# The sixteen extra tokens of an expert mixer: their copies, transposes and scalings placed behind query projection 9

## The chip, the cores and the metric

The kernel runs on one core of one Trainium2 chip. The metric is the device time of one execution in microseconds (us). The kernel before was timed three times: 1357.75 us in the median, 1357.3 to 1359.09.

## The reference

The reference computes one inference step of a hybrid decoder layer in float32, for 336 tokens of width 1024: 16 learned meta tokens and 256 prompt tokens of one sequence, and 8 running sequences of 8 tokens. A Conformer convolution branch and a Mamba-2 branch share an input projection; their gated sum goes through an output projection and is added to the input. The outputs include the new convolution caches and the recurrent states. Behind that stands the PEER expert mixer, which is the part that matters here:

```python
q = (xb @ w_q).reshape(T, PEER_HEADS, 2, D_KEY // 2)
s = jnp.einsum('thcd,hckd->thck', q, keys).astype(jnp.float32)
s1, i1 = lax.top_k(s[:, :, 0], PEER_TOPK)
s2, i2 = lax.top_k(s[:, :, 1], PEER_TOPK)
...
sc, f = lax.top_k(cand, PEER_TOPK)
...
g = jax.nn.softmax(sc, axis=-1)
act = jax.nn.gelu(jnp.einsum('thkd,td->thk', U[ids], xb).astype(jnp.float32), approximate=False)
w = (g * act).astype(xb.dtype)
return jnp.einsum('thk,thkd->td', w, V[ids])
```

Each token is normalised, projected to 8 heads of two 128-wide half queries, scored against 128 keys per half, and gets 16 of 16384 experts per head. Each chosen expert contributes a row of V, weighted by the softmax weight times the gelu of a dot product with a row of U. The result is added to the token and normalised once more. The outputs do not hold the meta tokens, so 320 tokens go through the mixer.

## The kernel before

**Stages.** The first 540 us or so compute the two branches and the output projection. Then come 16 query projections (one per head and half), with scores and top-16 searches, and then the experts. The 320 tokens are treated in two ways. For 176 of them (ND) the experts are computed densely: 128 blocks of U (`u_block`, L1274) give a matrix S of gelu values for all experts, which is masked with the softmax weights (`g_step`, L1303 to L1310), and 128 blocks of V are summed up in PSUM (`v_block`, L1368). For the other 144 tokens the chosen rows of U and V are gathered from HBM by indirect DMAs. 128 tokens (NGAT) sit one in each partition and take 128 gathers, one per head and choice. The last 16 tokens (NX), the extra tokens, sit in eight copies each in the 128 partitions (partition = copy x 16 + token), so that 16 further gathers serve all their 128 choices. 144 gathers in all, 1 MB each (L1085), each followed by a product with the token summed along the row (L1197), a gelu and a scaling (L1199, L1200), and a weighted sum (L1205).

**What the extra tokens need ahead of their gathers.** `x2e` holds the normalised extra tokens in eight copies, token by partition, and `acce` the sum that the gathers add to, at first zero except for the raw tokens in the first 16 partitions. The tokens lie feature by partition in `xT`. So POOL repeats 16 columns eight times into a 128 x 128 tile `xe` (L988, eight times, two buffers), PE transposes it into the PSUM tile `px` (L990, four into each of two tiles), ACT copies 16 partitions of it to `acce` (L991), and DVE scales it into `x2e` by the token's inverse norm and the weights row `n2r` (L992). The inverse norms are turned the same way: POOL copies them into `xe` (L979), PE multiplies by a column of the identity into column 3 of the PSUM tile `prs` (L981), and ACT copies that to `rsT` (L982). POOL also clears `acce` (L977). The gathered 128 tokens have the same steps ahead of these (L964 to L971), with columns 0 to 2 of `prs`.

**Query projections.** `weight` (L245) loads a 128 x 1024 slice of w_q by SP, ACT casts it to a high part `wh` (L219), and POOL takes the difference as a low part `wl` (L220, one in ten on DVE); `wh` and `wl` have two buffers each. `proj` runs 24 matmuls into a PSUM tile `pj` (L152, three buffers). ACT copies it to `qT` (L1104, three buffers). Three score matmuls (L1107) write the PSUM tile `psc`, one for each token tile, and ACT copies each out (L1109); for the gathered tokens DVE finds the top 16 at once (`top16`, L999 to L1007). Behind projections 7 and 15, `heads` turns the searches of four heads into expert numbers `gid` and weights `ggw`. Behind projection 7 the first four gathers are asked for (`ahead(0)`). The gathers' buffers `wuv` are five; `n2r` is held in one of them until its last reader is done.

**PSUM.** The tiles px, prs and psc all come from one tag with two buffers:

```python
def misc(shape, name):
    return ps.tile(shape, F32, name=name, tag="misc", bufs=2)
```

**Order.** The order on each engine is set when the program is built, by a planner that runs a model of the machine: at each moment an engine takes, among the instructions whose inputs and buffers are ready, the one that stands first in the program text. So work may be pulled ahead into gaps. On the chip each engine then runs its list strictly in order. In the stage in question the PE's order is left to the planner (`pin[0] = False`); in the branches before it, PE's order is that of the text.

Of the kernel before, what the change touches and what calls it, by code (L numbers as in the profile page):

```python
# [38 lines left out]
NX = 16  # L39
# [3 lines left out]
NCOL = NPICK + (NPICK // XQ if NX else 0)  # L43
XAT = 64
HG = 4
LEAD = 4
GT = 8
SB = 88
# [89 lines left out]
def body(tc, ia, oa, stop=None):  # L138
    nc = tc.nc
    with ExitStack() as top:  # L140
# [58 lines left out]
        def pj(name="pj"):  # L199
            return ps.tile([128, PJ], F32, name=name, tag="pj", bufs=3)[:, :T]  # L200

        def pj2(name="pj"):
            return pj(name)[:, :T2]
# [39 lines left out]
        def weight(src, i):  # L243
            raw = wp.tile([128, KD, 128], F32, name="wraw", bufs=rb[0])
            nc.sync.dma_start(raw, src[i].rearrange("p (k m) -> p k m", m=128))  # L245
            h = wp.tile([128, KD, 128], F32R, name="wh", bufs=2)
            l = wp.tile([128, KD, 128], F32R, name="wl", bufs=2)
            nw[0] += 1
            f_ = lm[0]
            on_dve = int((nw[0] + 1) * f_) > int(nw[0] * f_)  # L250
            split(h, l, raw, on_pool=not on_dve, on_dve=lm[0] == 1)
            return h, l
# [6 lines left out]
        def misc(shape, name):  # L259
            return ps.tile(shape, F32, name=name, tag="misc", bufs=2)  # L260
# [64 lines left out]
        p = misc([128, T], "pn1")  # L325
# [569 lines left out]
        for j in range(KD):  # L895
# [4 lines left out]
            p = pj2()  # L900
# [7 lines left out]
        for j in range(KD):  # L908
            w = weight(ia["w_o"], j)
            p = pj2()  # L910
# [13 lines left out]
        p = ps.tile([128, T], F32, name="pn2", tag="pb", bufs=1)  # L924
# [36 lines left out]
        for c_ in range(2):  # L961
            p = misc([128, 512], "px")
# [4 lines left out]
        p = misc([128, 4], "prs")  # L967
# [4 lines left out]
        for k in range(KD):  # L972
            nc.vector.scalar_tensor_tensor(nd[:, k, :], xT[:, k, NGAT:NGAT + ND], V("n2", k), rs2[:, NGAT:NGAT + ND],
                                           op0=OP.mult, op1=OP.mult)
        if NX:
            E0 = NGAT + ND
            nc.gpsimd.memset(acce, 0.0)  # L977
            xe = qp.tile([128, 128], F32, name="xe", bufs=2)
            nc.gpsimd.tensor_copy(xe.rearrange("p (q t) -> p q t", t=NX),  # L979
                                  rs2[:, None, E0:T2].to_broadcast([128, XQ, NX]))  # L980
            nc.tensor.matmul(p[:, 3:4], xe, ident[:, 0:1], start=True, stop=True)  # L981
            nc.scalar.copy(rsT[:, 3:4], p[:, 3:4])  # L982
            for c_ in range(2):
                p = misc([128, 512], "px")
                cs = slice(c_ * 512, c_ * 512 + 512)
                for k in range(4):
                    xe = qp.tile([128, 128], F32, name="xe", bufs=2)
                    nc.gpsimd.tensor_copy(xe.rearrange("p (q t) -> p q t", t=NX),  # L988
                                          xT[:, 4 * c_ + k, None, E0:T2].to_broadcast([128, XQ, NX]))
                    nc.tensor.transpose(p[:, k * 128:(k + 1) * 128], xe, ident)  # L990
                nc.scalar.copy(acce[:NX, cs], p[:NX])  # L991
                nc.vector.scalar_tensor_tensor(x2e[:, cs], p, rsT[:, 3:4], n2r[:, cs], op0=OP.mult, op1=OP.mult)  # L992
# [4 lines left out]
        def top16(vals, idx, v, h, late=False):  # L997
            L = v.shape[0]
            i_ = nc.vector.max(vals[:L, h, 0:8], v)  # L999
            if late:  # L1000
                tc.add_manual_dep(i_.ins, early[0], mybir.DependencyInfo(mybir.DependencyClass.NoSync,
                                                                         mybir.DependencyReason.DATA),
                                  reason="gathered tokens first")
            nc.vector.max_index(idx[:L, h, 0:8], vals[:L, h, 0:8], v)
            nc.vector.match_replace(v, vals[:L, h, 0:8], v, -3.0e38)
            nc.vector.max(vals[:L, h, 8:16], v)
            nc.vector.max_index(idx[:L, h, 8:16], vals[:L, h, 8:16], v)  # L1007
# [7 lines left out]
        def candidates(L, H_, s2):  # L1015
            c = kp.tile([128, PH * 136], F32, name="cand", bufs=1)[:L]
            cf = c[:, :H_ * 136].rearrange("p (h n) -> p h n", h=H_)
            nc.vector.tensor_tensor(cf[:, :, :16], s2[:, :, 0, 0:1].to_broadcast([L, H_, 16]), s2[:, :, 1, :],
                                    op=OP.add)
            nc.vector.tensor_tensor(cf[:, :, 16:].rearrange("p h (a b) -> p h a b", b=8),  # L1020
                                    s2[:, :, 0, 1:, None].to_broadcast([L, H_, 15, 8]),
                                    s2[:, :, 1, None, :8].to_broadcast([L, H_, 15, 8]), op=OP.add)
            return c, cf

        def table(L, H_, idx):
            sf = kp.tile([128, PH, 2, 16, 4], BF, name="sf", bufs=2)[:L, :H_]
            nc.vector.tensor_copy(sf.rearrange("p h c k t -> p (h c k) t"),
                                  idx.rearrange("p h k -> p (h k)")[:, :, None].to_broadcast([L, H_ * 32, 4]))
            return sf

        def places(L, H_, f):
            lo = kp.tile([128, PH * 16], U32, name="plo")[:L, :H_ * 16]
            rr = kp.tile([128, PH * 16], U32, name="prr")[:L, :H_ * 16]
            ab = [kp.tile([128, PH * 16], BF, name=f"pab{c_}")[:L, :H_ * 16] for c_ in range(2)]
            nc.vector.tensor_scalar(lo, f, 7, None, op0=OP.bitwise_and)
            nc.vector.tensor_scalar(rr, f, 3, None, op0=OP.logical_shift_right)
            nc.vector.tensor_scalar(ab[0], rr, 1.0, 0.0, op0=OP.subtract, op1=OP.max)
            nc.vector.tensor_scalar(ab[1], rr, 1.0, 8.0, op0=OP.is_equal, op1=OP.mult)
            nc.vector.tensor_tensor(ab[1], ab[1], lo, op=OP.add)
            return ab  # L1040
# [14 lines left out]
        def heads(h0):  # L1055
            hs_ = slice(h0, h0 + HG)
            cs = slice(16 * h0, 16 * (h0 + HG))
            sf = table(128, HG, si[0][:, 2 * h0:2 * h0 + 2 * HG])
            c, cf = candidates(128, HG, sv[0].rearrange("p (h c) k -> p h c k", c=2)[:, hs_])
            for h in range(HG):  # L1060
                top16(cv0, ci0, cf[:, h], h0 + h)
            ab = places(128, HG, ci0.rearrange("p h k -> p (h k)")[:, cs])
            pk = kp.tile([128, 2, HG * 16], F32, name="pkh")
            for half in range(2):
                look(pk[:, half], 128, HG, ab[half], sf, half, c)
            idf = kp.tile([128, HG * 16], F32, name="idh")
            nc.vector.scalar_tensor_tensor(idf, pk[:, 0], float(NK), pk[:, 1], op0=OP.mult, op1=OP.add)
            early.append(nc.vector.tensor_copy(gid[:, cs], idf).ins.name)
            g_ = kp.tile([128, HG, 16], F32, name="gh")
            nc.vector.tensor_tensor(g_, cv0[:, hs_], cv0[:, hs_, 0:1].to_broadcast([128, HG, 16]), op=OP.subtract)  # L1070
            act(g_, g_, AF.Exp, scale=rsT[:, 0:1])
            sm = kp.tile([128, HG], F32, name="smh")
            nc.vector.tensor_reduce(sm, g_, axis=AX.X, op=OP.add)
            nc.vector.reciprocal(sm, sm)
            nc.vector.tensor_tensor(ggw[:, cs].rearrange("p (h k) -> p h k", k=16), g_,
                                    sm[:, :, None].to_broadcast([128, HG, 16]), op=OP.mult)
# [6 lines left out]
        def gather(c):  # L1083
# [3 lines left out]
            steps = ustep[SB:] + vstep  # L1087
            if len(steps) > LEAD:
                tc.add_manual_dep(i_.ins, steps[-1 - LEAD], mybir.DependencyInfo(mybir.DependencyClass.Sync,
                                                                          mybir.DependencyReason.DATA),  # L1090
# [8 lines left out]
        for j in range(16):  # L1099
            w = weight(ia["w_q"], j)  # L1100
            p = pj()
            proj(p[:, :T2], w, rows(ah[:, :, :T2], al[:, :, :T2]))
            qT = qp.tile([128, T], F32, name="qT", bufs=3)
            nc.scalar.copy(qT[:, :T2], p[:, :T2])  # L1104
            p = misc([128, 3, NK], "psc")
            for i, (t0, L) in enumerate(KTILES):
                nc.tensor.matmul(p[:L, i], qT[:, t0:t0 + L], keys[:, j, :], start=True, stop=True)  # L1107
                s_ = sall[:, i - 1, j] if i else kp.tile([128, NK], F32, name="sco", bufs=9)
                nc.scalar.copy(s_[:L], p[:L, i])  # L1109
                if i == 0:  # L1110
                    top16(sv[i], si[i], s_[:L], j)
            if j % (2 * HG) == 2 * HG - 1:
                heads(j // 2 - HG + 1)
            if j == 2 * HG - 1:
                ahead(0)
# [386 lines left out]
```

## Time and profile before

| | |
|---|---|
| median of three runs | 1357.75 us (1357.3 to 1359.09) |
| the profiled execution | 1359.33 us |
| its span | 1357.6 us |
| PE busy | 1316.2 us (97%) |
| DVE busy | 1017.4 us (75%) |
| ACT busy | 526.4 us (39%) |
| POOL busy | 576.2 us (42%) |
| transferred | 382.05 MB, mean 281 GB/s |

The profile is of one execution. Its page gives busy times, the span in 40 slices and the chain of work that ended last; the trace behind it can be asked for stretches, for single tiles and lines, for who waited for whom, and for each engine's instructions in order of time. PE is TensorE's matmuls, PEld its weight loads, DVE VectorE, ACT ScalarE, POOL GpSimd, SP SyncE, which issues DMAs. A line "a<-b" means that the instruction writes a and reads b; L988 is line 988 of the kernel. An idle time in brackets is that of the engine ahead of the instruction, with what ended it. One float32 matmul stands as two instructions in the trace where its operands are plain float32 (psc, px, prs).

### The profile page before, as it was taken

Reading aid. Unit: us, or ns where it says so; the run is one execution under the profiler, and the core shown is the slowest. Engines: PE = TensorE matmul, PEld = TensorE weight load, DVE = VectorE, ACT = ScalarE, POOL = GpSimd, SP = SyncE. Lnnn points to the kernel's source line nnn. Section 1 sums busy time; section 2 is a strip of 40 time slices with the busy share of each in tenths; the row PEclk is TensorE's granted clock in tenths of the full one; section 3 lists DMA queues with packets and bytes.
Section 4 is the critical chain, followed back from the end, with each engine's and each line's share of the span. In section 5 each row is a group of like instructions: output and inputs, shape, how many; then the busy total and the mean of one; then the engine's idle time right before and its main releaser. Section 6 shows DMA issues by size and latency. Waiting matters only on the chain.

```text
span 1357.6 us, 24599 instructions
## 1 busy us (share of the span) xinstructions
PE 1316.2 (97%) x9324; PEld 1247.7 (92%) x9324; DVE 1017.4 (75%) x2340; ACT 526.4 (39%) x1393; POOL 576.2 (42%) x492
## 2 busy tenths in 40 slices
PE   9999999999999999999999998999999999989997
PEld 7888888888889999898998998999999999988997
DVE  7888777877877236789999986877877878765544
ACT  6777877778666444442232121121111101110012
POOL 2477776776665667542221331222222221332210
PEclk9899999999999999999999998999999999999999
DMA  6434554454343444628999999999999999999994
GB/s 239 156 125 168 169 176 129 148 166 172 128 138 126 156 144 155 193 94 316 392 415 412 394 415 414 374 409 378 379 403 415 386 375 383 382 417 414 415 415 170
DMA packets 87094, 382.05 MB, mean 281 GB/s; under 512 B 10144, under 2 KB 15648, under 8 KB 66368
## 3 DMA queue, kind: packets, MB, share of 16 engines
q1 hardware_dynamic: 65056, 227.46, 45.9%
q0 software_dynamic: 20736, 151.00, 27.5%
q10 hardware_dynamic: 1184, 2.02, 0.4%
q8 instruction: 73, 1.20, 0.4%
q14 instruction: 45, 0.37, 0.1%
HBM read 367.41 MB, written 13.03 MB: 280 GB/s over the span
## 4 chain that ended last, share of the span: by engine, by line
PE 74%; DVE 12%; DMA 11%; ACT 2%; issue 1%; POOL 0%; ACTq 0%; DVEq 0%; SPq 0%
PE pj L152 30%; PE va L1368 16%; PE pj L1274 14%; DMA eraw<-in_vE_dram 7%; PE pg L1303 4%; DMA eraw<-in_uT_dram 3%; PE pst L152 2%; DVE wuv L1197 1%; DVE ygat L1205 1%; PE po L152 1%; PE py L152 1%; DVE pcv L475 1%; PE pdec L152 1%; PE psc L1107 1%; PE ptr L157 1%
## 5 line engine op out<-in xcount | busy, mean ns | idle before, releaser
L1085 POOL DMA_INDIRECT wuv<-in_peer_uv_dram,gid x144 | 178.0, 1236 | 522.9 <-DVE ygat L1205 203.8
L1274 PE MATMUL pj<-nd,eraw 128*128 128x176 f32 x2048 | 324.1, 319 | 9.3 <-DMA eraw<-in_uT_dram 5.5
L220 POOL TENSOR_TENSOR wl<-wraw,wh 128x1024 fp32r<-128x1024 f32 x111 | 267.1, 2407 | 151.8 <-ACT wh L219 79.2
L1368 PE MATMUL va<-S,eraw 128*128 128x176 f32 x2048 | 315.5, 314 | 8.5 <-DMA eraw<-in_vE_dram 8.3
L1274 PEld LDWEIGHTS pj<-nd,eraw 128*128 128x128 f32 x2048 | 313.0, 194 | 11.5 <-ACT S L1276 6.2
L1368 PEld LDWEIGHTS va<-S,eraw 128*128 128x128 f32 x2048 | 306.0, 190 | 13.6 <-DMA eraw<-in_vE_dram 11.1
L152 PE MATMUL pj<-ah,wh 128*128 128x336 f32 (+1 forms) x768 | 244.4, 329 | 0.7 <-ACT xnf L195 0.7
L152 PE MATMUL pj<-al,wh 128*128 128x336 f32 (+1 forms) x768 | 234.5, 318 | 0.0
L1205 DVE SCALAR_TENSOR_TENSOR ygat<-wuv,scg,ygat 128x1024 f32<-128x1024 f32 x128 | 163.9, 1280 | 48.7 <-ACT scg L1200 48.5
L1199 ACT ACTIVATE scg<-scg 128x1 f32<-128x1 f32 x144 | 29.0, 202 | 429.3 <-DVE wuv L1197 429.2
L1197 DVE SCALAR_TENSOR_TENSOR wuv<-wuv,x2m 128x1024 f32<-128x1024 f32 x128 | 155.9, 1218 | 47.3 <-DMA wuv<-in_peer_uv_dram,gid 47.3
L219 ACT CAST wh<-wraw 128x1024 fp32r<-128x1024 f32 x125 | 131.1, 1050 | 117.6 <-PE pj L152 79.9
L475 DVE SCALAR_TENSOR_TENSOR pcv<-ccat,vec,pcv 128x256 f32<-128x256 f32 x464 | 148.7, 379 | 17.1 <-ACT pcv L473 17.1
L152 PEld LDWEIGHTS pj<-ah,wh 128*128 128x128 f32 x768 | 147.4, 192 | 8.6 <-ACT xnf L195 2.7
L152 PEld LDWEIGHTS pj<-al,wh 128*128 128x128 f32 x768 | 147.0, 192 | 0.7
L152 PE MATMUL pj<-ah,wl 128*128 128x336 f32 (+1 forms) x768 | 137.1, 316 | 0.0
L152 PEld LDWEIGHTS pj<-ah,wl 128*128 128x128 f32 x768 | 120.8, 189 | 0.8 <-issue 0.7
L1276 ACT ACTIVATE S<-pj 128x176 f32<-128x176 f32 x128 | 37.5, 311 | 141.8 <-PE pj L1274 141.7
L1303 PE MATMUL pg<-oh 128*128 128x64 bf16 x1056 | 75.0, 241 | 0.0
L1303 PEld LDWEIGHTS <-oh 128*128 128x128 bf16 x1056 | 70.9, 117 | 2.2
L1310 DVE TENSOR_TENSOR S<-S,pg 128x192 f32<-128x192 f32 (+1 forms) x66 | 31.6, 506 | 54.9 <-PE pg L1303 54.8
L489 DVE SCALAR_TENSOR_TENSOR pj<-mcat,vec,pj 128x360 f32<-128x360 f32 x96 | 56.2, 587 | 3.7 <-ACT pj L487 3.7
(366 smaller groups left out, 1701.7 us busy)
## 6 DMA issues: line engine op xcount, KB each, us to landing
eraw<-in_uT_dram SPq DMA_DIRECT2D x128, 512.0 KB, 10.0
eraw<-in_vE_dram SPq DMA_DIRECT2D x128, 512.0 KB, 11.3
wraw<-in_w_in_dram SPq DMA_DIRECT2D x80, 512.0 KB, 3.6
st<-in_state_dram SPq DMA_DIRECT2D x8, 1024.0 KB, 4.9
out_ssm_s_dram<-st SPq DMA_DIRECT2D x8, 1024.0 KB, 4.9
wraw<-in_w_mo_dram SPq DMA_DIRECT2D x16, 512.0 KB, 3.4
wraw<-in_w_q_dram SPq DMA_DIRECT2D x16, 512.0 KB, 3.4
wraw<-in_w_co_dram SPq DMA_DIRECT2D x8, 512.0 KB, 3.4
```

What stands on the lines that cost most here:

```text
L152: i_ = nc.tensor.matmul(*a_, **kw)
L219: (nc.vector.tensor_copy if on_dve else nc.scalar.copy)(h, src)
L220: (nc.gpsimd if on_pool else nc.vector).tensor_tensor(l, src, h.bitcast(F32), op=OP.subtract)
L475: t = nc.vector.scalar_tensor_tensor(o, i_, wv, a_, op0=OP.mult, op1=OP.add)
L489: nc.vector.scalar_tensor_tensor(o, cat[:, w:w + n], wv, o, op0=OP.mult, op1=OP.add)
L1085: i_ = nc.gpsimd.indirect_dma_start(out=u, out_offset=None, in_=ia["peer_uv"], in_offset=bass.IndirectOffsetOnAxis(ap=gid[:, c:c + 1], axi ...
L1197: nc.vector.scalar_tensor_tensor(u[:, :D], u[:, :D], 1.0, x2m if c < NPICK else x2e, op0=OP.mult, op1=OP.mult, accum_out=w)
L1205: nc.vector.scalar_tensor_tensor(a_, u[:, D:], scg[:, c:c + 1], a_, op0=OP.mult, op1=OP.add)
L1274: i_ = nc.tensor.matmul(p[:, :ND], raw[:, k, :], nd[:, k, :], start=(k == 0), stop=(k == KD - 1))
L1276: nc.scalar.activation(Sv(b), p[:, :ND], AF.Gelu)
L1303: i_ = nc.tensor.matmul(pg[:, q, :], B[:, q // 4, :, q % 4], A[:, c_, q // 4, :, q % 4], start=(c_ == 0), stop=(c_ == 2))
L1368: i_ = nc.tensor.matmul(va[k // 2][:, k % 2], raw[:, k, :], Sv(b), start=False, stop=(b == 127), skip_group_check=True)
```

## The change

The block for the extra tokens becomes a function, and is called in the loop over the 16 projections when j is 9, behind the scores of projection 9 and ahead of the text of projection 10. It asks for a `prs` tile of its own, where before it used column 3 of the one that holds the other scales.

```diff
+EXTRA = 9
...
-        if NX:
+        def extra_tokens():
             E0 = NGAT + ND
             nc.gpsimd.memset(acce, 0.0)
             xe = qp.tile([128, 128], F32, name="xe", bufs=2)
             nc.gpsimd.tensor_copy(xe.rearrange("p (q t) -> p q t", t=NX),
                                   rs2[:, None, E0:T2].to_broadcast([128, XQ, NX]))
+            p = misc([128, 4], "prs")
             nc.tensor.matmul(p[:, 3:4], xe, ident[:, 0:1], start=True, stop=True)
             nc.scalar.copy(rsT[:, 3:4], p[:, 3:4])
             for c_ in range(2):
                 p = misc([128, 512], "px")
                 cs = slice(c_ * 512, c_ * 512 + 512)
                 for k in range(4):
                     xe = qp.tile([128, 128], F32, name="xe", bufs=2)
                     nc.gpsimd.tensor_copy(xe.rearrange("p (q t) -> p q t", t=NX),
                                           xT[:, 4 * c_ + k, None, E0:T2].to_broadcast([128, XQ, NX]))
                     nc.tensor.transpose(p[:, k * 128:(k + 1) * 128], xe, ident)
                 nc.scalar.copy(acce[:NX, cs], p[:NX])
                 nc.vector.scalar_tensor_tensor(x2e[:, cs], p, rsT[:, 3:4], n2r[:, cs], op0=OP.mult, op1=OP.mult)
...
                 if i == 0:
                     top16(sv[i], si[i], s_[:L], j)
+            if j == EXTRA:
+                extra_tokens()
             if j % (2 * HG) == 2 * HG - 1:
                 heads(j // 2 - HG + 1)
```

## The prediction

> **What bounds the kernel now.** I read the stages first (busy time, clock and transfer rate by stretch), then the chain of waits through the stretch that the change touches, then the order of instructions on PE, ACT and POOL there.
>
> The stages; columns are the stretch, its length, busy time with instruction counts of PE, PE's weight load, DVE, ACT and POOL, the granted clock, the DMA share and GB/s:
>
> ```profile
> 558.00:568.00 10.00, 10.00 (x69) 9.79 (x70) 9.78 (x11) 4.69 (x9) 6.64 (x7) 1.00 0.65 211
> 568.00:575.00 7.00, 3.97 (x22) 2.65 (x20) 3.17 (x15) 2.89 (x8) 3.69 (x6) 0.84 0.47 150
> 575.00:580.00 5.00, 5.00 (x22) 5.00 (x22) 3.31 (x20) 0.66 (x2) 0.00 (x0) 0.54 0.00 0
> 580.00:600.00 20.00, 20.00 (x134) 18.35 (x132) 17.16 (x114) 9.48 (x26) 9.58 (x4) 1.00 0.28 87
> 600.00:623.00 23.00, 23.00 (x155) 21.48 (x155) 22.46 (x104) 8.60 (x25) 9.57 (x4) 1.00 0.50 159
> 646.00:763.00 117.00, 112.85 (x724) 111.96 (x723) 116.22 (x383) 29.72 (x96) 28.25 (x23) 0.96 1.00 401
> 763.00:830.00 67.00, 61.44 (x455) 60.60 (x456) 54.79 (x84) 14.01 (x61) 24.34 (x18) 0.99 1.02 416
> 830.00:1169.00 339.00, 339.00 (x2791) 335.22 (x2792) 261.10 (x418) 49.17 (x190) 78.23 (x67) 0.99 0.99 390
> 1169.00:1331.00 162.00, 153.50 (x1010) 149.27 (x1008) 91.23 (x111) 18.34 (x73) 40.93 (x31) 1.00 1.02 412
> ```
>
> From 646 on the transfers are nearly always full (401 to 416 GB/s, 390 while PE is full); the total of bytes behind that point is fixed. So the end moves with the moment at which that saturated stretch begins. Ahead of it lies the query projection stage (about 545 to 623), where DMA is mostly idle, PE is full from 580, and PE is neither full nor at its clock from 568 to 580. The chain of waits (start, us, what) goes right through this hole:
>
> ```profile
> 568.99 2.34 POOL wl L220
> 571.33 0.24 POOL xe L988
> ...
> 571.94 0.25 PE psc L1107 x2
> ...
> 575.31 4.79 PE pj L152 x19
> ...
> 591.84 2.94 PE pj L152 x20
> ...
> 601.28 0.28 DVE sv L999
> ...
> 622.73 0.10 DVE gid L1068
> ...
> 645.68 38.82 PE pj L1274 x240
> ```
>
> The reader should see three things. From 568.99 to 571.57 the chain leaves PE, which has no projection left that it may start and sits behind a transpose of the extra tokens (px L990, in the next rows) that waits for a POOL copy (xe L988) queued behind a weight split (wl L220). After that, 19 projection matmuls take 4.79 us where 20 take 2.94 us at 591.84. And from 601.28 the chain runs on DVE, through the top-16 searches of the eighth score block to the expert numbers (gid, 622.73), which the gathers need, and on to the dense blocks (pj L1274). So the gather stream is fed by the score blocks, and those were late.
>
> Why they were late: two PSUM buffers (tag misc) serve the token transposes (px), the column of scales (prs) and the scores (psc). In program order the extra tokens' prs column and two px tiles stand ahead of score block 0. Three projections (pj buffers) and three transposed queries (qT buffers) may wait; then PE stops. The rows for this, PE then ACT:
>
> ```profile
> 571.61 0.33 PE L990 MATMUL px<-cst,xe 128*128 128x128 f32 x1 [2.43 <-POOL xe L988]
> 572.53 0.59 PE L1107 MATMUL psc<-keys,qT 128*128 128x128 f32 x2 [0.25 <-ACT sco L1109]
> 574.51 0.80 PE L1107 MATMUL psc<-keys,qT 128*128 128x128 f32 x2 [0.35 <-ACT sall L1109]
> 618.75 0.40 PE L152 MATMUL pj<-ah,wh 128*128 128x320 f32 x1
> ```
>
> ```profile
> 557.31 1.07 ACT L965 COPY ygat<-px 128x512 f32<-128x512 f32 x2 [3.74 <-DVE vec L216]
> 574.36 0.42 ACT L1104 COPY qT<-pj 128x320 f32<-128x320 f32 x1
> 617.33 0.42 ACT L1104 COPY qT<-pj 128x320 f32<-128x320 f32 x1
> ```
>
> The copy at 574.36 is the fourth query copy; until then no projection buffer came free again.
>
> **The change part by part.** What moves, with the count and cost of each (min/median/max ns, first and last start):
>
> ```profile
> L988 POOL COPY xe<-xT x8: 289/294/427, 558.6 to 572.3; 128x128 f32<-128x128 f32 x8
> L990 PE MATMUL px<-cst,xe x8: 270/318/421, 561.6 to 573.1; 128*128 128x128 f32 x8
> L981 PE MATMUL prs<-cst,xe x2: 166/208/250, 568.2 to 568.2; 128*128 128x1 f32 x2
> L979 POOL COPY xe<-vec x1: 479/479/479, 558.2 to 558.2; 128x128 f32<-128x128 f32 x1
> L977 POOL MEMSET acce<- x1: 953/953/953, 557.3 to 557.3; 128x1024 f32 x1
> L991 ACT COPY acce<-px x2: 575/575/575, 569.2 to 573.6; 16x512 f32<-16x512 f32 x2
> L992 DVE SCALAR_TENSOR_TENSOR x2e<-px,rsT,wuv x2: 741/745/749, 569.8 to 574.7; 128x512 f32<-128x512 f32 x2
> ```
>
> Nothing is added or dropped but the reservation of one more PSUM tile for the prs column. No DMA is among the moved instructions. The work stays: POOL 0.95 + 0.48 + 8 x 0.29 = 3.8 us, DVE 2 x 0.745 = 1.5 us, ACT 2 x 0.575 = 1.15 us and one copy of a single column, and ten short PE matmuls, whose cost is the same in either place. What changes is what they hold up.
>
> *Gain 1, the idle.* With the extra tokens gone from the front, score block 0 can take the PSUM buffer that the ygat copies (from 557.31, two in 1.07 us) free at about 558, instead of starting at 571.94. Query copy 3 then follows the first score block instead of coming at 574.36, and PE does not run out of work. Gone: 2.43 + 0.25 + 0.35 = 3.0 us of PE idle.
>
> *Gain 2, the clock.* The granted clock is 0.54 from 575 to 580. At the 2.94/20 = 0.147 us of the row at 591.84 the 19 matmuls would take 2.8 us; they took 4.8: 2.0 us. Together 5.0 us.
>
> [...]
>
> *Cost behind projection 9.* The trace shows no such place, so it is bounded. Below: nothing, because POOL is idle between splits there (rows below: 1.89 and 2.37 us before each 2.4 us split), room for copies of 0.29 us, and PE has projections to run meanwhile. Above: the same PE wait and clock drop as at the front, 2.43 + 2.0 = 4.4 us, since behind a POOL split a copy can be late again. I take one exposed copy, 0.3 us, because the row nearest is POOL's gap in that very stage, which is longer than the copy. DVE's 1.5 us ride in stalls of its own: it was busy 3.17 of 7 and 3.31 of 5 us in the hole, waiting for scores that now come early. If that cover is gone, gid is 1.5 us later, and the gathers with it.
>
> ```profile
> 600.24 2.38 POOL L220 TENSOR_TENSOR wl<-wraw,wh 128x1024 fp32r<-128x1024 f32 x1 [1.89 <-PE pj L152]
> 605.00 2.40 POOL L220 TENSOR_TENSOR wl<-wraw,wh 128x1024 fp32r<-128x1024 f32 x1 [2.37 <-ACT sall L1109]
> 623.12 1.15 POOL L1085 DMA_INDIRECT wuv<-in_peer_uv_dram,gid  x1 [6.67 <-DVE sv L999]
> ```
>
> *Does the gain arrive?* Queued behind the moved POOL copies are the splits of projections 10 to 15 and then the gathers (623.12, after 6.67 us of waiting on DVE); the splits have the gaps above, the gathers wait for gid. The buffer that holds the weights row n2 is one of the five wuv buffers that the gathers use; it is now given back only after the moved x2e scalings. Four gathers are asked for ahead of them, so only a fifth could wait, and projection 9 ends well ahead of gid. Late next after the hole is the DVE search chain from 601.28 to 622.73: it starts when score block 7 arrives, so it moves with the scores. Then everything behind moves as one: blocks, gathers, and the transfers.
>
> Sum: -3.0 - 2.0 + 0.3 = -4.7 us. The profiled execution took 1359.33 us with a span of 1357.6; it would take 1354.6 with a span of 1352.9. The median shown is 1357.75, 1.6 below the profiled execution, so the forecast is 1357.75 - 4.7 = 1353.0 us.
>
> **The rivals.**
>
> *More than the hole.* DVE idled 0.22 + 3.83 + 1.69 + 2.84 + 0.54 = 9.1 us between 558 and 623 (length less busy in the five rows). If early scores let it search in all of that, gid comes 9 us sooner. For it: DVE carries the chain from 601. Against: the dense blocks still start only when PE is through its projections, and PE too is near full from 646 to 763 (112.85 of 117). Time: 1357.75 - 9.1 = 1348.6.
>
> *Hidden anyway, or spent again.* The stretch 763 to 830 waits on transfers; if the gathers' start is set by DVE's whole load (22.46 of 23 us busy from 600) and not by the arrival of scores, PE is early and then waits. Or the extra tokens cost the upper bound of 4.4 us in the new place: -5.0 + 4.4 = -0.6. Time: 1357.2 to 1357.75. Against: the chain enters DVE from PE at 601.28.
>
> *The planner puts it back.* Instructions are ordered by a planner that fills gaps with any ready work; the copies are ready at 558. It could place the extra tokens at the front again: 1357.75. Against: score blocks 0 to 2 are ready too when the PSUM buffers come free, and now stand first.
>
> *Slower: the score chain is held in mid-stage.* Behind projection 9 the two misc buffers are shared with a score chain that has almost no credit: projection 15 starts at 618.75, and the pj buffer it needs is given back by the copy that starts at 617.33 and takes 0.42 us (the fourth from the last of 16), so 1.0 us before. At the front credit was plenty, all buffers being empty. If the px tiles hold the buffers as they did there (first transpose 561.6, last scaling over at 575.4: 13.8 us, over two buffers 6.9 us) PE idles 6.9 - 1.0 = 5.9 us, and with the clock drop 7.9 us; less the 5.0 gained, +2.9 us: 1360.7. It decides from the point where the score chain is held by more than 1.0 + 5.0 - 2.0 = 4.0 us. For it: these buffers and this slack. Against: in the front the tiles were held long because splits and projections were queued between the copies; the first two copies can now be made long before, and PE takes the transposes as they come.
>
> **How the numbers follow.** A measurement of this kernel can tell about 0.2%, 2.7 us, from no change. Forecast 0.45 (1353.0, its own range 1351 to 1356), more than the hole 0.16, hidden or spent 0.17, put back 0.07, slower 0.15. Faster by over 2.7 us: most of the first (0.42) and the second (0.16), 0.58. Same: the third and fourth and a remainder of the first, 0.27. Slower by more than 2.7 us: 0.15, the fifth case, whose price is just beyond that bound. The range runs from just under the figure for more than the hole to between no change and the slower case, 1348.0 to 1359.8; it leaves out most of the slower case and the far side of the other.
>
> **What would show it.** Right: in the changed profile the first score matmul (psc L1107) starts near 558 to 560, not 571.9; no PE gap at 569 to 575 and no clock of 0.54 behind it; gid near 617; the dense blocks near 641 instead of 645.7; every later stage about 5 us sooner with equal rates. The copies xe L988 lie around projections 8 to 10, with PE waits of at most 0.5 us. Wrong: a new PE gap with px or psc behind projection 9 (the slower case, or the spent one), gid at 622 with PE early (hidden), or xe still at 558 to 572 (put back). A changed order in the dense blocks, outside the moved work, would be a cause that I have not priced.

## The result, and the profile after

The changed kernel took 1351.74 us in the median of five runs (1348.87 to 1352.57), against 1357.75 for the kernel before: 6.0 us less by the medians. The ratio of the two kernels is given as 0.9941, with a 95% interval of 0.9926 to 0.9957 (5.8 to 10.0 us); it isn't the quotient of the two medians, which is 0.9956 and lies at the interval's near end. Faster was forecast, with 1353.0. The profiled execution took 1349.96 us with a span of 1348.2, 9.4 us below the profiled one of before; single executions lie up to 3.7 us apart here, so that difference is not the gain.

The stages of the changed kernel, in the columns of the prediction's first view:

```profile
558.00:568.00 10.00, 10.00 (x70) 9.43 (x69) 9.76 (x20) 4.66 (x12) 4.68 (x2) 1.00 0.55 180
568.00:575.00 7.00, 6.87 (x47) 6.42 (x47) 6.83 (x39) 2.90 (x10) 5.64 (x2) 1.00 0.45 145
575.00:580.00 5.00, 5.00 (x38) 5.00 (x37) 5.00 (x34) 1.38 (x3) 2.21 (x1) 1.00 0.34 113
580.00:600.00 20.00, 20.00 (x134) 18.21 (x132) 17.98 (x110) 9.50 (x24) 9.77 (x5) 1.00 0.37 111
600.00:623.00 23.00, 21.25 (x143) 20.21 (x142) 21.54 (x94) 5.17 (x12) 11.08 (x13) 1.00 0.73 255
646.00:763.00 117.00, 107.56 (x695) 106.32 (x694) 116.31 (x380) 28.81 (x95) 26.35 (x22) 0.95 0.99 391
```

The hole is gone: PE is full from 568 to 580 at a clock of 1.00, and DVE works there (6.83 of 7 and 5.00 of 5 us, before 3.17 and 3.31). What was not looked for stands in the last row: PE has less busy time from 646 to 763 (107.56 of 117, before 112.85), and DVE is full there in both kernels (116.31 of 117 us, before 116.22).

The changed kernel's chain of waits, and then the score matmuls (psc) and the moved instructions (counts, min/median/max ns, first and last start; these lines of the kernel stand two further down than before; each of the eight px transposes is one instruction in the trace, each score matmul two):

```profile
556.99 0.34 PE psc L1109 x2
...
592.18 0.28 DVE sv L1001
...
612.45 0.23 DVE idh L1069
...
613.19 8.56 DMA wuv<-in_peer_uv_dram,gid
```

```profile
L1109 PE MATMUL psc<-keys,qT x96: 270/275/377, 556.8 to 639.3; 128*128 128x128 f32 x64, 128*64 128x128 f32 x32
L990 POOL COPY xe<-xT x8: 286/294/696, 557.0 to 619.1; 128x128 f32<-128x128 f32 x8
L992 PE MATMUL px<-cst,xe x8: 270/272/332, 607.1 to 621.4; 128*128 128x128 f32 x8
L994 DVE SCALAR_TENSOR_TENSOR x2e<-px,rsT,wuv x2: 722/725/728, 616.5 to 628.1; 128x512 f32<-128x512 f32 x2
```

Score block 0 starts at 556.8 instead of 571.8; DVE enters the chain at 592.18 instead of 601.28; the first gather is issued at 613.19 instead of 623.12. (Some 1.6 us of each lay ahead of the stage in this execution: the `ygat` copies of 557.31 start at 555.72 here.) Of the extra tokens only the first copies are made early. The transposes run from 607 to 621, and the second x2e scaling starts at 628.1, well behind the place in the text. The fifth gather, which the prediction said could wait for this scaling, is issued at 626.88, 9.75 us after the fourth.

### The profile page after: what moved, and what is told of

Same layout as the page of the kernel before. It is cut to its first block, busy times and chain, and to the rows that moved or that the text cites. A ratio compares the mean times of both kernels' runs of the same rounds, so it can differ in the third digit from the quotient of the medians.

```text
span 1348.2 us, 24591 instructions
## 1 busy us (share of the span) xinstructions
PE 1312.1 (97%) x9324; PEld 1243.1 (92%) x9324; DVE 1016.2 (75%) x2340; ACT 526.1 (39%) x1393; POOL 569.7 (42%) x492
## 4 chain that ended last, share of the span: by engine, by line
PE 74%; DVE 14%; DMA 10%; ACT 2%; issue 0%; ACTq 0%; DVEq 0%
PE pj L153 31%; PE va L1372 17%; PE pj L1278 13%; DMA eraw<-in_vE_dram 7%; PE pg L1307 5%; DVE ygat L1209 2%; DVE wuv L1201 2%; PE pst L153 2%; DMA eraw<-in_uT_dram 2%; PE po L153 1%; PE py L153 1%; PE pdec L153 1%; DVE cand L1052 1%; DMA wuv<-in_peer_uv_dram,gid 1%; PE ptr L158 1%; PE pq L153 1%
## 5 line engine op out<-in xcount | busy, mean ns | idle before, releaser
L1087 POOL DMA_INDIRECT wuv<-in_peer_uv_dram,gid x144 | 170.9, 1186 | 524.4 <-DVE ygat L1209 157.1
```

The costliest lines, as they stand in the source:

```text
L1087: i_ = nc.gpsimd.indirect_dma_start(out=u, out_offset=None, in_=ia["peer_uv"], in_offset=bass.IndirectOffsetOnAxis(ap=gid[:, c:c + 1], axi ...
```

## The experiments

Every kernel was timed against the kernel before on its own chip. Three numbers of each profile are added: when the first expert numbers are cast (gid), when the first dense block is written to S, and how long DVE idled from 558 to 763 (length less busy time). Times in a profile count from the start of its span, and the stage itself starts up to 1.8 us earlier in some executions than in others, by the `ygat` copies; so differences of a microsecond or two between two kernels' gid or S mean little.

| kernel | median us | ratio, 95% interval | gid | S | DVE idle |
|---|---|---|---|---|---|
| before | 1357.75 | 1 | 622.6 | 645.3 | 9.9 |
| changed | 1351.74 | 0.9941, 0.9926 to 0.9957 | 612.7 | 639.8 | 4.6 |
| front_own_psum | 1351.6 | 0.9957, 0.9942 to 0.9972 | 615.8 | 638.3 | 3.6 |
| mid_own_psum | 1352.26 | 0.9959, 0.9944 to 0.9974 | 616.2 | 638.4 | 4.7 |
| extra_left_out | 1350.39 | 0.9941, 0.9923 to 0.9958 | 613.3 | 635.7 | 5.2 |
| front_eight_queries | 1362.71 | 1.0032, 1.0015 to 1.0048 | 629.3 | 636.9 | 21.0 |
| behind_projection_0 | 1355.38 | 0.9976, 0.9963 to 0.9989 | 621.5 | 644.6 | 7.8 |
| behind_projection_4 | 1356.9 | 0.9990, 0.9978 to 1.0002 | 619.8 | 639.8 | 9.7 |
| behind_projection_12 | 1353.62 | 0.9962, 0.9949 to 0.9976 | 614.7 | 646.0 | 3.3 |
| behind_projection_15 | 1352.81 | 0.9946, 0.9927 to 0.9966 | 615.1 | 644.3 | 3.5 |
| first_gather_late | 1351.49 | 0.9948, 0.9933 to 0.9962 | 614.0 | 642.3 | 5.6 |
| gathers_late | 1363.46 | 1.0032, 1.0021 to 1.0044 | 612.9 | 645.8 | 3.4 |
| score0_own_psum | 1361.86 | 1.0023, 1.0011 to 1.0035 | 614.9 | 647.6 | 3.3 |
| five_us_more_on_dve | 1358.11 | 1.0005, 0.9996 to 1.0014 | 612.7 | 639.4 | 3.4 |

**Is it the PSUM buffers or the place?** The extra tokens stay at the front, in other PSUM buffers:

```diff
+            p = ps.tile([128, 4], F32, name="prs", tag="pb", bufs=1)
             nc.tensor.matmul(p[:, 3:4], xe, ident[:, 0:1], start=True, stop=True)
...
-                p = misc([128, 512], "px")
+                p = ps.tile([128, 512], F32, name="px", tag="y", bufs=2)
```

> The kernel before, with the extra tokens' work at the front as it was, but its prs column and its two px tiles in other PSUM buffers (tags pb and y, idle in this stage), so that the scores have the two misc buffers to themselves. Theory A (the extra tokens cost because they hold the two PSUM buffers that score block 0 needs): the gain of the change without the move, 1351 to 1354 us; first score matmul near 558, no PE gap at 569 to 575, gid near 613 to 617. Rival B (the place is what costs: POOL copies between the first splits, transposes between the first projections): 1356 to 1359, and the gap stays.

Measured 1351.6 us, ratio 0.9957. Its stages, and its scores and extra copies:

```profile
568.00:575.00 7.00, 7.00 (x50) 6.46 (x48) 6.55 (x31) 3.72 (x9) 4.08 (x5) 1.00 0.35 104
575.00:580.00 5.00, 5.00 (x36) 4.83 (x36) 4.90 (x29) 2.45 (x8) 2.12 (x3) 1.00 0.50 170
```

```profile
L1108 PE MATMUL psc<-keys,qT x96: 270/275/377, 558.0 to 637.8; 128*128 128x128 f32 x64, 128*64 128x128 f32 x32
L989 POOL COPY xe<-xT x8: 281/298/407, 558.2 to 576.8; 128x128 f32<-128x128 f32 x8
```

The copies still run between the first weight splits, 558 to 577, and the hole is gone all the same; the gain is the changed kernel's, within the intervals. So it was the two PSUM buffers, not the place. The same tags for the changed kernel:

> The changed kernel (extra tokens behind projection 9), with the same other PSUM buffers for prs and px. Theory A with nothing more to pay behind projection 9: as the changed kernel, within 1.5 us of 1351.7. Rival (the tiles hold up scores 10 to 15 in the new place, and that reaches the end): 2 to 5 us below the changed kernel, 1347 to 1350.

1352.26 us: no better than the change. What the px tiles hold up in the changed kernel (their second scaling starts at 628.1) doesn't reach the end by anything that these runs can tell. The fifth gather follows the fourth by 1.2 us there instead of 9.75, and that doesn't show in the time either. The next kernel leaves the work out, so that the results of the sixteen extra tokens are missing:

```diff
-            xe = qp.tile([128, 128], F32, name="xe", bufs=2)
...
-                nc.vector.scalar_tensor_tensor(x2e[:, cs], p, rsT[:, 3:4], n2r[:, cs], op0=OP.mult, op1=OP.mult)
+            nc.gpsimd.memset(x2e, 0.0)
```

> The changed kernel without the extra tokens' copies, transposes and scalings at all: x2e and acce are only cleared, so the outputs of the sixteen extra tokens are left out; their 16 gathers, products and sums stay. Theory A: the moved work costs nearly nothing where it now stands, 0 to 1.5 us below the changed kernel (1350.2 to 1351.7). Rival (it is still paid behind projection 9): 2 to 5 us below, 1347 to 1350.

1350.39 us, 1.4 below the changed kernel by the medians, but with the same ratio, 0.9941. The two scalings are 1.45 us of DVE work (2 x 0.725). So the moved work costs little where it now stands; whether it costs its own DVE time or nothing at all, these runs can't tell.

**Is it PE's idle time and clock?** The kernel before, with more buffers for the queries, so that PE need not stop:

```diff
-            qT = qp.tile([128, T], F32, name="qT", bufs=3)
+            qT = qp.tile([128, T], F32, name="qT", bufs=8)
```

> The kernel before with eight buffers for the transposed queries in place of three: PE cannot run out of projections behind projection 5, while score block 0 still waits for the PSUM buffers until about 570. If PE's idle time and its clock are the whole gain: 1351 to 1353. If the lateness of the scores, and so of gid and the gathers, is what reaches the end: 1355 to 1358, with PE full but gid still near 620.

1362.71 us, ratio 1.0032: slower than before. Its stages:

```profile
558.00:568.00 10.00, 10.00 (x72) 9.79 (x71) 8.17 (x7) 5.01 (x11) 6.29 (x6) 1.00 0.63 198
568.00:575.00 7.00, 7.00 (x51) 6.98 (x50) 0.75 (x1) 3.07 (x5) 5.39 (x7) 1.00 0.41 138
575.00:580.00 5.00, 5.00 (x38) 4.98 (x36) 2.57 (x10) 2.19 (x5) 3.20 (x2) 1.00 0.52 182
580.00:600.00 20.00, 20.00 (x135) 18.68 (x134) 13.99 (x89) 8.44 (x20) 11.12 (x5) 1.00 0.35 108
600.00:623.00 23.00, 23.00 (x153) 21.17 (x152) 19.08 (x115) 5.29 (x20) 2.39 (x1) 1.00 0.66 212
```

PE is full at full clock in every row, with the 5.0 us of the prediction's two gains in hand, and the time went up. The gain doesn't last even on PE: from 558 to 763 it was busy for 193.68 us here, for 194.19 in the kernel before and for 190.47 in the changed one. DVE stands still instead: 0.75 of 7 us; score block 0 starts even later than before, at 575.1, and gid comes at 629.3. The test isn't pure, since it delays the scores as well. But it shows that PE's time at the front doesn't bring the gain by itself, and that what got worse, the scores and DVE's idle time, weighs more.

**Does the start of the gathers set the end?** A POOL addition that reads gid stands ahead of the first gathers:

```diff
+                late = qp.tile([128, 2560], I32, name="late")
+                nc.gpsimd.tensor_tensor(late, gid[:, 0:1].to_broadcast([128, 2560]), gid[:, 0:1].to_broadcast([128, 2560]), op=OP.add)
                 ahead(0)
```

> The changed kernel with one POOL addition of 2560 elements per partition that reads gid and stands ahead of the first four gathers (its result is used by nobody). It should take about 6 us, by the 2.4 us of the splits of 1024. If the start of the gathers reaches the end, the kernel is later than the changed one by most of the addition's length, 1355 to 1358, and the transfer share from 610 to 625 falls. If gathers have slack there: 1351 to 1353.

POOL's order in that kernel:

```profile
614.23 4.45 POOL L1120 TENSOR_TENSOR late<-gid 128x2560 int32<-128x2560 int32 x1 [3.41 <-DVE gid L1070]
618.85 1.15 POOL L1087 DMA_INDIRECT wuv<-in_peer_uv_dram,gid  x1 [0.17 <-issue]
```

The addition took 4.45 us, not the 6 expected. The first gather is issued at 618.85 against 613.19 in the changed kernel; 1.2 of these 5.7 us lay ahead of the stage, so the delay is about 4.4 us. The time is the same within the intervals, 1351.49 (a full 4.4 us would have been a ratio near 0.997, outside this run's interval). So the start of the first gathers has slack. An earlier form with six POOL copies was meant to do the same:

```diff
+                late = qp.tile([128, 1024], F32, name="late")
+                for _ in range(6):
+                    nc.gpsimd.tensor_copy(late, gid[:, 0:1].to_broadcast([128, 1024]))
```

> The changed kernel with six copies of 128 x 1024 elements on POOL that read gid and stand ahead of the first four gathers: the gathers start later by their length (about 6 us), all else stays. Theory A2: the end is later by most of that, 1355 to 1358. Rival (PE's projections and dense blocks set the end, the gathers have slack): 1351 to 1353.

It did something else: the planner put one copy ahead of the gathers (first issue 614.4) and five between later ones. 1363.46 us, which I can't put down to a start that hardly moved; of this below.

**Is it DVE?** The changed kernel with more DVE work that nobody needs:

```diff
+                more = qp.tile([128, D], F32, name="more")
+                for _ in range(4):
+                    nc.vector.scalar_tensor_tensor(more, x2m, gid[:, 0:1].bitcast(F32), x2m, op0=OP.mult, op1=OP.mult)
                 ahead(0)
```

> The changed kernel with four more DVE products of 128 x 1024 behind the first expert numbers (they read gid, and nobody uses their result), about 1.2 us each by the row of the products with the gathered rows: 4.9 us more of DVE work in the stretch in which DVE is busy all the time (623 to 763). Theory D (DVE's backlog up to 763 is what the late scores cost, and what the change shortens): the end is later by 4 to 5 us than the changed kernel's 1351.7, 1355.5 to 1357. Rival (transfers and PE set the end there, and DVE has slack): 1351 to 1353.

1358.11 us: 6.4 us more than the changed kernel by the medians, and the whole gain is gone (ratio 1.0005). The added rows, and the stage that follows:

```profile
L1121 DVE SCALAR_TENSOR_TENSOR more<-x2m,gid x4: 1259/1262/1268, 613.5 to 624.7; 128x1024 f32<-128x1024 f32 x4
```

```profile
646.00:763.00 117.00, 106.80 (x695) 106.01 (x694) 116.42 (x399) 30.57 (x95) 30.01 (x22) 0.96 0.97 381
```

4 x 1.262 = 5.0 us of DVE work cost at least that much. gid and S are where they were (612.7 and 639.4), and POOL's instructions stand in the same order. DVE has a backlog of searches and gather products: its first pause of over half a microsecond behind 646 comes at 763.3 in the changed kernel and at 776.6 here. So the DVE time lost ahead of that was not made up in this run. Why the end moves by more than 5.0 us is open; from about 800 on the planner also ordered dense blocks and masking differently on PE here, and that wasn't tested apart.

**How far back may they stand?** `EXTRA` is 0, 4, 12 and 15 in place of 9.

> The changed kernel with the extra tokens called behind projection 0 instead of 9: score block 0 stands ahead of them, all others behind. Theory A2: scores 1 to 7 are held up as all were before, gid between the two kernels, 1353 to 1357. Rival (only the first score block matters, since the query buffers are then moving): 1350 to 1353.

> The changed kernel with the extra tokens called behind projection 4. If each score block of the first eight that stands behind the extra tokens is late by them, gid lies between that behind projection 0 (621.5) and that behind projection 9 (612.7), and the end at 1352 to 1355. If the planner pulls them ahead wherever a PSUM buffer is free, it is as behind projection 9: 1350 to 1352.

> The changed kernel with the extra tokens called behind projection 12: all eight first score blocks stand ahead of them, as behind projection 9. gid as there (612 to 616), the end at 1350 to 1353. A rival by which the place matters further: above 1354.

> The changed kernel with the extra tokens called behind projection 15. Theory A2: nothing of the scores behind gid is held up earlier, gid as in the changed kernel; scores 10 to 15 come earlier, the release of the buffer under S may come later: 1350 to 1354. Rival (what the tiles hold up behind projection 9 is a cost that reaches the end): 1347 to 1350.

Behind 12 and 15 the gain is that of 9, within the intervals. Behind 0 about 0.24% is left of it, as the first theory had it, and behind 4 none that can be told from zero, which neither had. The kernel with 4: its stage, its longest wait of DVE, and the next score matmul and search behind it:

```profile
580.00:600.00 20.00, 18.07 (x116) 15.89 (x116) 12.72 (x75) 9.12 (x23) 10.47 (x12) 1.00 0.33 106
```

```profile
DVE x2e L994 <- ACT acce L993: 5.5, 1, 5.5
```

```profile
591.67 0.49 PE L1109 MATMUL psc<-keys,qT 128*128 128x128 f32 x2 [1.34 <-DVE x2e L994]
592.50 0.29 DVE L1001 MAX8 sv<-sco 128x8 f32<-128x128 f32 x1 [0.88 <-ACT sco L1111]
```

The first x2e scaling waits 5.5 us, until the px tile is full and ACT has copied from it. No search stands ready meanwhile: between 582.3 and 591.67 PE starts no score matmul, and the next one waits until the scaling has read the px tile; the next search then waits for the copy of its scores. So the px tile holds up the scores as it did at the front, and DVE (12.72 of 20 us busy) has nothing to search. This is the prediction's slower rival, a score chain held in mid-stage; PE idles 1.9 of the 20 us and DVE 7.3.

**Still earlier scores?** The changed kernel, with the scores of the gathered tokens in a PSUM tile of their own:

```diff
+            p0 = ps.tile([128, NK], F32, name="ps0", tag="y", bufs=2)
...
-                nc.tensor.matmul(p[:L, i], qT[:, t0:t0 + L], keys[:, j, :], start=True, stop=True)
+                nc.tensor.matmul(p[:L, i] if i else p0[:L], qT[:, t0:t0 + L], keys[:, j, :], start=True, stop=True)
...
-                nc.scalar.copy(s_[:L], p[:L, i])
+                nc.scalar.copy(s_[:L], p[:L, i] if i else p0[:L])
```

> The changed kernel, with the scores of the gathered tokens (token tile 0 of each projection) in a PSUM tile of their own (tag y, two buffers) instead of the first third of the misc tile that they share with the scores of tiles 1 and 2. Theory A2 (what reaches the end is how early the eight score blocks of tile 0 lie on DVE, and with them gid and the first gather): gid 2 to 6 us before the 612.7 of the changed kernel, and the end as much earlier, 1346 to 1350. Rival (PE's idle and clock were the whole gain, and nothing is left to gain by earlier scores): 1351 to 1353.

Neither came true: gid did not come earlier (614.9), and the time is 1361.86. From 600 to 646 PE idled 8.3 us (length less busy), S is first written at 647.6, and by 830 only 70 dense blocks are written to S, against 74 before and 75 in the changed kernel.

**What stays open.** In the table the time goes with DVE's idle time up to 763 (five_us_more_on_dve's 3.4 leaves out its 5.0 us of useless work), with two exceptions: gathers_late and score0_own_psum have little of it (3.4 and 3.3 us) and are slower. By 900, 95 and 93 dense blocks are written to S in them, against 97 before and 98 in the changed kernel; score0_own_psum is behind by 830 already. On PE the order of dense blocks and masking differs in them from about 800 on, but so it does in first_gather_late, which takes no longer than the changed kernel. The cause is open.

The bytes that were moved sort the kernels as well. From 558 to 763 the rate was 322 to 331 GB/s in all kernels at 1350 to 1354 us, and 315 to 319 in those above 1355, with gathers_late (325) as the one exception. The kernel before has 315, the changed one 326: some 2 MB more, or two gathers, and DVE has finished the products of 26 gathers by 763 instead of 24. A gather needs a `wuv` buffer that DVE has finished with (in the kernel before, POOL stood idle for 203.8 us ahead of gathers until a sum of DVE's, `ygat`, was done), so DVE's time and the transfers rise and fall together here. five_us_more_on_dve shows that a delay on DVE reaches the end (its rate is 319); whether it gets there through DVE's own work or through the transfers, no run parts.

front_eight_queries lost 11.1 us of DVE time and only 4.3 us at the end (0.32% of 1357.75); that its S came 8.4 us sooner is a likely offset, not a shown one.

## Why the prediction was right, and where it was not

The mechanism at the front was right: the two PSUM buffers held back score block 0, and everything fed by the scores came late. Score block 0 was expected at 558 to 560 and started at 556.8; the gap and the clock of 0.54 are gone; dense blocks near 641 were expected, S is first written at 639.8; gid was expected near 617 and came at 612.7. Some 1.6 us of each lay ahead of the stage. That the buffers are the cause, and not the place, front_own_psum shows. That the time lies in the range says less: 1348.0 to 1359.8 holds no change at all as well.

The size was short: -4.7 was forecast, -6.0 measured by the medians, with an interval that begins at -5.8. The step that failed is the pricing by the two gains, PE's idle 3.0 us and PE's clock 2.0 us. front_eight_queries has both in full at the front and is slower, and in the changed kernel itself PE has no more busy time by 763 than before. The term that the runs support in its place is the one that I gave to the rival "more than the hole": DVE's idle time. It fell from 9.9 to 4.6 us up to 763, 5.3 us, and five_us_more_on_dve shows that such time reaches the end. The rival priced all 9.1 us of the stage; the changed kernel still leaves 2.0 us from 580 to 600 and 1.5 from 600 to 623. That both sums came to about 5 is luck: PE and DVE stood still for the same late scores, but nothing makes the two lengths equal.

A statement under it was too simple: that the end moves with the moment at which the transfers become full, set by when the first gathers start. first_gather_late moves the first gathers by about 4.4 us at no cost that its interval shows. The bytes moved by 763 do go with the time, as said, so that the transfers themselves aren't ruled out. The row of 646 to 763 that the prediction quotes held a second candidate, DVE busy 116.22 of 117 us, and I read only the GB/s of it.

The cost behind projection 9 was taken as 0.3 us on PE, with waits of at most 0.5 us. PE didn't wait there at first, but the second px tile was finished only at 628, behind the first gathers, later than the prediction had it. Among the last scores PE then waited 2.07 us and, for that tile's scaling, 1.17 us (the matmuls at 623.78 and 628.92). This cost nothing that mid_own_psum could recover. The 1.5 us of DVE work that was said to ride in DVE's stalls does so at most in part: the second scaling runs where DVE is full (17.00 of 17 us from 623 to 640). What that costs at the end is not shown; without it the median is 1.4 us lower and the ratio the same. The slower rival, a score chain held in mid-stage, is real, but at projection 4. The planner didn't put the work back.

## What to carry to other kernels

A hole in the fullest engine may be the mark of a stall that costs another engine its time. Before pricing it there, look for the engine that is full in the stretch behind, and count what that one loses in the hole. Work of known length, added to one engine, tells whether its time reaches the end. And when tiles with different urgency share a few PSUM buffers, the order in the program decides who waits: score block 0 started at 571.8 us behind the px tiles and at 556.8 ahead of them. Buffers that idle in that stage did as well as a move here (0.9957 against 0.9941, within the intervals).

## What was not expected of the hardware

In the kernel before, PE gaps of 2.43 and 0.25 us were followed by a granted clock of 0.50 from 573 on (the prediction's 0.54 is the mean from 575 to 580); the third gap, 0.35 us, came after the fall. In the changed kernel this PE gap (in brackets) left the clock at 1.00 in the stretch around it:

```profile
623.78 0.43 PE L1109 MATMUL psc<-keys,qT 128*64 128x128 f32 x2 [2.07 <-ACT sall L1111]
```

```profile
623.00:640.00 17.00, 13.97 (x80) 11.28 (x80) 17.00 (x75) 7.55 (x30) 6.24 (x4) 1.00 1.02 419
```

PE idled 3.0 us there in all, in pieces. It isn't that the step lies between 2.07 and 2.43 us: in behind_projection_0 gaps of 1.21 and 0.35 us were followed by a clock of 0.53 from 576 to 580:

```profile
575.14 0.49 PE L1109 MATMUL psc<-keys,qT 128*128 128x128 f32 x2 [1.21 <-DVE x2e L994]
```

So in these runs the length of a gap alone doesn't tell whether the clock falls, and no bound comes out of them.
